# A two-layer trunk on one core: the FFN as two stages with its inner rows in DRAM between them

## Chip, cores, metric

One core of a Trainium2 chip runs one launch of the kernel. The metric is device time in microseconds (us). Engines are named as the profile names them: PE multiplies matrices (PEld loads its weights), DVE, ACT and POOL work on tiles, SP issues most DMAs.

## What is computed

The reference runs two layers over 1024 latent tokens and 128 prompt tokens (T = 1152, that is 9 tiles of 128), with D = 1024. Each layer is a mixer (layer 0: a diagonal state-space part and differential attention; layer 1: a gated short convolution and an RG-LRU) and a gated convolutional FFN. Every part is wrapped in norms:

```python
def _pre(x, m, g, j):
    return rmsnorm(x, g) * (1 + m[:, 3 * j + 1, None]) + m[:, 3 * j, None]

def _post(x, y, m, g, j):
    return x + m[:, 3 * j + 2, None] * rmsnorm(y, g)
```

The FFN multiplies the normed rows by `ffn_w_up` (1024 x 5632), convolves each of the 5632 columns along the tokens with three taps, takes gelu of the first 2816 columns times the others (the inner rows: 22 blocks of 128), and multiplies them by `ffn_w_down` (2816 x 1024). All is float32.

## The kernel before

Every operand of a product is split into a high and a low part of PE's float32 type, and three products (high·high, high·low, low·high) replace one (`mm3`, L81 to L87). Everything up to the output gate of layer 0's mixer, some 790 us, is the same instructions before and after; the change is in `phase_c`, which runs layer 0's `mixer_out`, its FFN, `mixer1` (layer 1's mixer), `mixer_out` again and layer 1's FFN.

- `ffn` (L1349 on) takes one inner block of the 22 at a time: two column blocks of `ffn_w_up`, each in three chunks of 384 to 386 tokens (24 products a chunk, 72 a block), convolution straight from PSUM on ACT (L1371) and DVE (L1374), gelu (L1389), the product of the halves (L1392) and its split into `mh` and `ml` (L1393, L1394).
- `down` (L1410 on) is called for two inner blocks at a time, while the next blocks are in work, and adds two halves of 512 columns for each token tile into nine accumulators `acc` in SBUF (L1420). 
- `ffn_end` (L1424 on) runs over the nine tiles after the last `down`: sum of squares (`junk`, L255), root on POOL (`rsv`, `rs`: L141, L144), scale by the gate table (L1447), add the residual row (L1448), store; in layer 0 also the next norm (square again, root `q`, L277), eight transposes on PE (`tps`, L284), eight identities on ACT that write `h` (L287) and its split on DVE (L289) and POOL (L290).
- `mixer1` (L1468 on) makes 20 column blocks from `w_in_cd` in three chunks of 384. Four of them feed the RG-LRU (`lru_branch`): the block goes through a four-tap convolution (L1485), is split into `xh` and `xl`, and is multiplied by gate matrices into `gps` tiles; sigmoids (L1526), tanh, exp and root on ACT, and a scan along the tokens on DVE (L1547 forwards, L1550 backwards) follow. The buffer of the first gate, `r`, is the same in both directions.
- `mixer_out` multiplies by the output weights (`ops`), then post norm, residual, store, and the FFN's pre norm.

PSUM: four tiles of one bank for `pps` and `ops` (`ps`), two for `dps` and `gps` (`pd`), two for transposes (`pt`). The text of the program gives only dependencies: a scheduler at build time writes each engine's order, and each engine then runs its instructions, and starts its DMAs, strictly in that order.

## Time and profile before

| | us |
|---|---|
| median of 3 runs (2998.35 to 3001.52) | 3000.33 |
| span of the profiled execution | 2997.2 |
| PE busy | 2816.8 (94%) |
| DVE busy | 2035.9 (68%) |
| ACT busy | 1096.7 (37%) |
| PE busy between 800 and 1700 us | 898.67 of 900 |

The span is what the profile covers; it is 3.1 us under the median of the runs. The chain that ended last, followed back, tells what an engine's time is worth: an engine that is busy but not on the chain costs nothing. The granted clock of PE (1.00 is 2.4 GHz, 0.50 is 1.2 GHz) is given for a stretch as a mean.

### The profile page before, as it was taken

What the parts mean: (1) busy time and instruction counts of PE and PEld (TensorE: products, weight loads), DVE (VectorE), ACT (ScalarE), POOL (GpSimd) and SP (SyncE); (2) the same over time, 40 slices, a digit from 0 to 9 for tenths busy, and PEclk for the clock granted to TensorE, in tenths of its full rate; (3) what the DMA queues carried; (4) which work ended last, traced back from release to release, by engine and by line L of the source; (5) the groups of instructions that cost most, each with busy time, mean ns of one, the idle gap of its engine ahead of it and who ended that gap; (6) DMA issues with size and microseconds to landing.
All of it is one profiled execution on the core that took longest, in us unless ns stands there. A gap on an engine that the chain in (4) does not pass through costs nothing.

```text
span 2997.2 us, 40584 instructions
## 1 busy us (share of the span) xinstructions
PE 2816.8 (94%) x15196; PEld 2557.3 (85%) x15196; DVE 2035.9 (68%) x3572; ACT 1096.7 (37%) x1921; POOL 813.7 (27%) x982
## 2 busy tenths in 40 slices
PE   7976788888999999999999989999999999999998
PEld 3874566777789999999999979997899999999997
DVE  6777765988668888888655685455455555555557
ACT  5222113766454222322222365554532222222222
POOL 2699972877131000000000151112300000000001
PEclk9998899999999999999999999999999999999999
DMA  6434447552642333323211131124411111111113
GB/s 222 142 86 107 117 138 200 137 116 75 193 146 89 98 99 96 97 91 93 62 43 57 64 122 55 53 88 146 138 46 43 43 43 43 43 43 43 43 36 134
DMA packets 298835, 279.45 MB, mean 93 GB/s; under 512 B 45454, under 2 KB 259682, under 8 KB 298638
## 3 DMA queue, kind: packets, MB, share of 16 engines
q1 hardware_dynamic: 266168, 238.51, 25.8%
q0 software_dynamic: 14912, 23.21, 3.1%
q10 hardware_dynamic: 17558, 15.14, 1.8%
q8 instruction: 119, 1.95, 0.3%
q14 instruction: 78, 0.64, 0.1%
HBM read 220.59 MB, written 56.20 MB: 92 GB/s over the span
## 4 chain that ended last, share of the span: by engine, by line
PE 69%; DVE 6%; ACT 3%; issue 2%; DMA 1%; POOL 1%; ACTq 0%; DVEq 0%; POOLq 0%; SPq 0%
PE pps L87 43%; PE dps L87 16%; PE ops L87 6%; DVE e L1077 1%; DVE nb L1060 1%; PE sA L1055 1%; ACT e L1066 1%; PE gps L87 1%; PE tps L284 1%; DVE wh L1102 0%; DVE s L1114 0%; PE ops L1145 0%; DMA mw<-w_mod 0%; POOL hl L290 0%; PE gps L759 0%
## 5 line engine op out<-in xcount | busy, mean ns | idle before, releaser
L87 PE MATMUL pps<-hh,whi 128*128 128x384 f32 (+1 forms) x2880 | 977.0, 339 | 1.1 <-ACT whi L97 0.7
L87 PE MATMUL pps<-hh,wlo 128*128 128x384 f32 (+1 forms) x2880 | 974.7, 339 | 2.2 <-DVE wlo L99 2.2
L87 PE MATMUL pps<-hl,whi 128*128 128x384 f32 (+1 forms) x2880 | 974.7, 339 | 0.6 <-POOL hl L798 0.4
L87 PEld LDWEIGHTS pps<-hh,whi 128*128 128x128 f32 x2880 | 546.1, 190 | 17.5 <-issue 3.2
L87 PEld LDWEIGHTS pps<-hh,wlo 128*128 128x128 f32 x2880 | 545.6, 189 | 15.2 <-DVE wlo L99 3.2
L87 PEld LDWEIGHTS pps<-hl,whi 128*128 128x128 f32 x2880 | 546.4, 190 | 8.1 <-DVE hl L798 0.7
L99 POOL TENSOR_TENSOR wlo<-wr,whi 128x1024 fp32r<-128x1024 f32 x44 | 109.2, 2487 | 1455.3 <-PE dps L87 1162.5
L1374 DVE SCALAR_TENSOR_TENSOR cc<-pps,cvc,cc 128x255 f32<-128x255 f32 (+1 forms) x704 | 342.0, 511 | 145.0 <-ACT cc L1371 139.8
L1420 DVE TENSOR_TENSOR acc<-acc,dps 128x512 f32<-128x512 f32 x360 | 245.9, 683 | 232.5 <-PE dps L87 231.5
L1371 ACT ACTIVATE cc<-pps,cvc 128x383 f32<-128x383 f32 (+2 forms) x264 | 175.0, 665 | 414.1 <-PE pps L87 393.3
L87 PE MATMUL dps<-whi,mh 128*128 128x512 f32 x792 | 311.8, 394 | 1.2 <-DVE acc L1420 1.2
L87 PE MATMUL dps<-whi,ml 128*128 128x512 f32 x792 | 312.0, 394 | 0.0
L87 PE MATMUL dps<-wlo,mh 128*128 128x512 f32 x792 | 310.5, 392 | 0.0
L97 ACT ACTIVATE whi<-wr 128x1024 fp32r<-128x1024 f32 x168 | 177.7, 1059 | 278.3 <-PE pps L87 196.6
L99 DVE TENSOR_TENSOR wlo<-wr,whi 128x1024 fp32r<-128x1024 f32 x124 | 153.9, 1243 | 85.4 <-PE pps L87 70.4
L231 DVE SCALAR_TENSOR_TENSOR macc<-mw,sil,macc 128x256 f32<-128x256 f32 x392 | 174.9, 482 | 18.9 <-DMA mw<-w_mod 18.1
L87 PEld LDWEIGHTS dps<-whi,ml 128*128 128x128 f32 x792 | 148.8, 188 | 33.7
L87 PEld LDWEIGHTS dps<-whi,mh 128*128 128x128 f32 x792 | 149.2, 188 | 20.8 <-DVE acc L1420 2.4
L87 PEld LDWEIGHTS dps<-wlo,mh 128*128 128x128 f32 x792 | 149.2, 188 | 18.8
L1389 ACT ACTIVATE cc<-cc 128x385 f32<-128x385 f32 x132 | 69.3, 525 | 248.1 <-DVE cc L1374 232.2
L1104 POOL TENSOR_TENSOR wl<-wf,wh 128x512 fp32r<-128x512 f32 (+2 forms) x96 | 144.4, 1523 | 52.5 <-DVE ra L1074 44.1
L1394 DVE TENSOR_TENSOR ml<-cc,mh 128x385 fp32r<-128x385 f32 x132 | 118.2, 899 | 34.2 <-ACT mh L1393 34.2
(356 smaller groups left out, 4171.6 us busy)
## 6 DMA issues: line engine op xcount, KB each, us to landing
wr<-ffn_w_up SPq DMA_DIRECT2D x88, 512.0 KB
mw<-w_mod SPq DMA_DIRECT2D x224, 128.0 KB
x<-x SPq DMA_DIRECT2D x45, 512.0 KB
wr<-ffn_w_down SPq DMA_DIRECT2D x44, 512.0 KB
wm<-w_mod SPq DMA_DIRECT2D x40, 512.0 KB
k<-kh POOLq DMA_DIRECT2D x8, 1408.0 KB, 6.4
wr<-w_in_cd SPq DMA_DIRECT2D x20, 512.0 KB
yr<-y SPq DMA_DIRECT2D x17, 512.0 KB
```

Of the source, the lines that this page charges most:

```text
L87: nc.tensor.matmul(ps, x, y, start=first and i == 0 and j == 0, stop=last and i == n - 1 and j == 2)
L97: nc.scalar.activation(hi, raw, AF.Copy)
L99: (eng or nc.vector).tensor_tensor(lo, raw, f(hi), op=OP.subtract)
L231: nc.vector.scalar_tensor_tensor(acc[v], wt, s, acc[v], op0=OP.mult, op1=OP.add)
L284: nc.tensor.transpose(ps[:, i], tmp[:, b * 128:(b + 1) * 128], self.id)
L1055: pin(nc.tensor.matmul(A[:, c:c + w], heads[u.h, 2][:, m, u.q0:u.q0 + 128], heads[u.h, m][:, j, u.k0 + c:u.k0 + c + w], start=j == 0, stop ...
L1104: pin((nc.vector if late else nc.gpsimd).tensor_tensor(vl, u.wf[b][:, :k], f(vh), op=OP.subtract))
L1371: nc.scalar.activation(cc[:, :no], ps[:, q:q + no], AF.Identity, bias=cw[3], scale=cw[1])
L1374: nc.vector.scalar_tensor_tensor(cc[:, oa - o0:ob - o0], ps[:, oa + d - i0:ob + d - i0], cw[j], cc[:, oa - o0:ob - o0], op0=OP.mult, op1=O ...
L1389: nc.scalar.activation(cc[:, :no], cc[:, :no], AF.Gelu_apprx_tanh)
L1394: nc.vector.tensor_tensor(ml[:, o0:o1], g[1][:, :no], f(mh[:, o0:o1]), op=OP.subtract)
L1420: nc.vector.tensor_tensor(acc[t][:, sl], acc[t][:, sl], ps, op=OP.add)
```

## The change

The FFN becomes two stages. `up` makes all 22 inner blocks: each column block in two halves of 576 tokens, each half two products of 288 columns for every weight (96 a block), in a PSUM tile of two banks. DVE and ACT copy it to SBUF (tile `C`), the convolution runs from there over all tokens, and the inner rows go to DRAM (`m0`, `m1`), unsplit. `down` then takes groups of 8, 8 and 6 inner blocks. For each group it keeps the split weights in SBUF, and for each tile loads the group's inner rows (`mr`), splits them (`mh` on ACT, `ml` on DVE), and makes all products of the tile in one PSUM tile: 48 matmuls of 512 columns in the first two groups, 36 in the last. Group 0 copies the result to `acc` on ACT, the others add it on DVE (1024 wide). In the last group `finish` is called for each tile: what `ffn_end` did, per tile. The 28 pieces of the modulation, which stood in layer 0's `ffn`, stand 22 in `up` and 6 in group 0 of `down`.

Pools: `big` has 14 tiles (normed rows, split weights of `down`, RG-LRU buffers), `mid` 8, and `wr` 8 tiles, which raw weights, their split pairs in `up`, `mr`, `mh`, `ml`, residual rows, `tmp` and tables share. PSUM: three tiles of two banks for every product (`pps`, `gps`, `ops`, `dps` alike), two for transposes. `mixer1` makes its 20 blocks in the same two halves of 576.

```diff
-    def ffn(self, l, hh, hl, acc, back):
...
-    def down(self, grp, acc, w_down):
...
-    def ffn_end(self, acc, xin, ga, out=None, xout=None, cols=None, hh=None, hl=None):
...
+    def pair(self, raw, eng, pool=None):
+        shape = list(raw.shape)
+        p = (pool or self.wr).tile([128, 2] + shape[1:], F32R, tag="big" if pool else "wr", name=self.nm("wp"))
+        self.nc.scalar.activation(p[:, 0], raw, AF.Copy)
+        eng.tensor_tensor(p[:, 1], raw, f(p[:, 0]), op=OP.subtract)
+        return p
+    def prod(self, prs, ys, name):
+        nc = self.nc
+        ps = self.bank2(name)
+        w = HT // 2
+        steps = [(p[:, x, k], y[j][:, k]) for p, y in zip(prs, ys) for k in range(4) for x, j in ((0, 0), (0, 1), (1, 0))]
+        for n, (x, y) in enumerate(steps):
+            for c in range(2):
+                nc.tensor.matmul(ps[:, c, :w], x, y[:, c * w:c * w + w], start=n == 0, stop=n == len(steps) - 1)
+        return ps[:, :, :w]
...
+    def up(self, l, H, back):
+        nc = self.nc
+        w_up = self.a["ffn_w_up"][l]
         for fb in range(NFB):
+            C = []
+            for b in (fb, NFB + fb):
+                raw = self.load_w(w_up[:, b * 128:b * 128 + 128].rearrange("(k p) c -> p k c", p=128), [128, 8, 128])
+                C.append(self.mid_tile([128, 2, HT], "C"))
+                prs = [self.pair(raw[:, q * 4:q * 4 + 4], (nc.gpsimd, nc.vector)[q]) for q in range(2)]
+                for n in range(2):
+                    pv = self.prod(prs, [H.b[q, n] for q in range(2)], "pps")
+                    if n:
+                        nc.scalar.activation(two(C[-1][:, n]), pv, AF.Copy)
+                    else:
+                        nc.vector.tensor_copy(two(C[-1][:, n]), pv)
+            self.up_rest(l, fb, C)
             if back:
                 self.mod_piece(*back.pop(0))
+    def up_rest(self, l, fb, C):
...
+        nc.vector.tensor_tensor(g[1], g[0], g[1], op=OP.mult)
+        nc.sync.dma_start(self.scratch(f"m{l}", [NFB, 128, T])[fb], g[1])
...
+    GROUPS = (range(0, 8), range(8, 16), range(16, 22))
+    def down(self, l, finish, back):
+        nc = self.nc
+        w_down = self.a["ffn_w_down"][l]
+        m = self.scratch(f"m{l}", [NFB, 128, T])
+        acc = []
+        for gi, fbs in enumerate(self.GROUPS):
+            n = len(fbs)
+            W = []
+            for fb in fbs:
+                W.append(self.pair(self.load_w(w_down[fb * 128:fb * 128 + 128], [128, D]), nc.gpsimd if fb % 2 else nc.vector, self.big))
+            for t in range(NT):
+                raw = self.wr_tile([128, n, 128], "mr")
+                nc.sync.dma_start(raw, m[fbs[0]:fbs[-1] + 1, :, t * 128:t * 128 + 128].rearrange("f p t -> p f t"))
+                hi, lo = (self.wr_tile([128, n, 128], "m" + x, F32R) for x in "hl")
+                nc.scalar.activation(hi, raw, AF.Copy)
+                nc.vector.tensor_tensor(lo, raw, f(hi), op=OP.subtract)
+                ps = self.bank2("dps")
+                for i in range(n):
+                    for j, (x, y) in enumerate(((hi, 0), (lo, 0), (hi, 1))):
+                        for h in range(2):
+                            nc.tensor.matmul(ps[:, h], x[:, i], W[i][:, y, h * 512:h * 512 + 512],
+                                             start=i == 0 and j == 0, stop=i == n - 1 and j == 2)
+                pv = ps.rearrange("p h c -> p (h c)")
+                if gi == 0:
+                    acc.append(self.mid_tile([128, D], "acc") if t < 8 else self.wr_tile([128, D], "acc"))
+                    nc.scalar.activation(acc[t], pv, AF.Copy)
                 else:
+                    nc.vector.tensor_tensor(acc[t], acc[t], pv, op=OP.add)
+                if gi < 2 and back:
+                    self.mod_piece(*back.pop(0))
+                if gi == 2:
+                    finish(t, acc[t])
+    def ffn_fin(self, t, y, xin, ga, out=None, xout=None, cols=None, H=None):
+        nc = self.nc
+        x = self.wr_tile([128, D], "x")
+        nc.sync.dma_start(x, xin[t * 128:t * 128 + 128])
+        tmp = self.wr_tile([128, D], "tmp")
+        rs = self.rstd(self.sumsq([y], tmp), D)
+        nc.vector.scalar_tensor_tensor(y, y, rs, ga[t == 8], op0=OP.mult, op1=OP.mult)
+        nc.vector.tensor_tensor(y, y, x, op=OP.add)
+        nc.sync.dma_start(out(t) if out else xout[t * 128:t * 128 + 128], y)
+        if out is None:
+            self.pre(t, y, tmp, cols, H)
...
         def P(c0, use):
-            self.proj(self.wcol(w, c0), hh, hl, self.ps, "ps", CH, use)
+            raw = self.load_w(w[:, c0:c0 + 128].rearrange("(k p) c -> p k c", p=128), [128, 8, 128])
+            p = self.pair(raw, V, self.big)
+            for n in range(2):
+                use(self.prod([p[:, :, q * 4:q * 4 + 4] for q in range(2)], [H.b[q, n] for q in range(2)], "pps"), n * HT, n * HT + HT)
...
-                    for i0, i1 in CH:
-                        ps = self.pd.tile([128, 512], F32, tag="pd", name=self.nm("gps"))
-                        self.mm3(ps[:, :i1 - i0], [(Wg[0][:, d * 2 + src], Wg[1][:, d * 2 + src])], [(xh[:, i0:i1], xl[:, i0:i1])])
-                        s = A.activation(dst[:, i0:i1], ps[:, :i1 - i0], AF.Sigmoid, bias=col(bc + d * 4 + j))
+                    for n in range(2):
+                        ps = self.bank2("gps")[:, :, :HT // 2]
+                        xv, lv = (two(x[:, n * HT:n * HT + HT]) for x in (xh, xl))
+                        for i, (u, y) in enumerate(((0, xv), (0, lv), (1, xv))):
+                            for c in range(2):
+                                nc.tensor.matmul(ps[:, c], Wg[:, u, d * 2 + src], y[:, c], start=i == 0, stop=i == 2)
+                        s = A.activation(two(dst[:, n * HT:n * HT + HT]), ps, AF.Sigmoid, bias=col(bc + d * 4 + j))
                 t = A.activation(t_, r, AF.Tanh, scale=self.hc[:, d * 4 + j:d * 4 + j + 1])
...
-            self.A = P("A", 1)
-            self.C1, self.wr, self.w, self.whi, self.C2 = P("C1", 1), P("wr", 2), P("w", 4), P("whi", 5), P("C2", 1)
-            self.cv, self.nrm = P("cv", 4), P("nrm", 2)
+            self.big = P("big", 14)
...
-            self.mid = P("mid", 6)
-            self.B = P("B", 1)
-            self.ps = P("ps", 4, space=PSUM)
-            self.pd = P("pd", 2, space=PSUM)
+            self.mid, self.wr = P("mid", 8), P("wr", 8)
+            self.ps = P("ps", 3, space=PSUM)
             self.pt = P("pt", 2, space=PSUM)
...
+            fin = {}
+            def finish0(t, y):
+                if t == 0:
+                    fin["ga"] = [self.table(self.wr, "wr", 0, 5, v) for v in range(2)]
+                    fin["cols"] = self.mod_cols(1, (1, 0), self.wr, "wr", self.pt, "pt", 2)
+                    fin["H"] = Blocks(self, False)
+                self.ffn_fin(t, y, x1, fin["ga"], None, x2, fin["cols"], fin["H"])
             with self.P("mp", 1) as self.mp, self.P("rp", 2) as self.rp:
-                self.ffn(0, hh, hl, acc, back)
+                self.up(0, H, back)
+                self.down(0, finish0, back)
             assert not back
-            self.junk = P("junk", 1).tile([128, D], F32, name="junk")
-            GA = lambda l: [[self.table(self.whi, "whi", l, 5, 0)], [self.table(self.cv, "cv", l, 5, 1, h, 512) for h in (0, 512)]]
-            hh, hl = H()
-            ga = GA(0)
-            cols = self.mod_cols(1, (1, 0), self.nrm, "n", self.pt, "pt", 2)
-            self.ffn_end(acc, x1, ga, None, x2, cols, hh, hl)
...
+            self.up(1, H, [])
+            gb = []
+            def finish1(t, y):
+                if t == 0:
+                    gb.extend(self.table(self.wr, "wr", 1, 5, v) for v in range(2))
+                self.ffn_fin(t, y, x3, gb, lambda t: self.o["o_ys"][0, t * 128:t * 128 + 128] if t < 8 else self.o["o_yp"][0])
+            self.down(1, finish1, [])
```

The order that the scheduler wrote, at three places. First PE in `mixer1`, at the gates of the second RG-LRU block: `pps` are products of a column block, `gps` of a gate matrix, `xh` and `xl` the two parts of the convolved block. Before:

```order
L87 MATMUL pps_18013<-hh_16681,wlo_17985 128x384
L87 MATMUL pps_18013<-hh_16681,whi_17983 128x384
L87 MATMUL gps_17815<-xh_17794,whi_17790 128x384
L87 MATMUL gps_17815<-xl_17795,whi_17790 128x384
L87 MATMUL gps_17815<-xh_17794,wlo_17792 128x384
L87 MATMUL gps_17820<-xh_17794,whi_17790 128x384
L87 MATMUL gps_17820<-xl_17795,whi_17790 128x384
L87 MATMUL gps_17820<-xh_17794,wlo_17792 128x384
L87 MATMUL pps_18013<-hl_16682,whi_17983 128x384
L87 MATMUL pps_18013<-hh_16681,wlo_17985 128x384
L87 MATMUL pps_18013<-hh_16681,whi_17983 128x384
```

After (each row x2 is two matmuls):

```order
L1408 MATMUL pps_18258<-hl_16730,wp_18205 128x288 x2
L1408 MATMUL pps_18258<-hh_16729,wp_18205 128x288 x2
L1578 MATMUL gps_18332<-xh_18321,wp_18318 128x288 x2
L1578 MATMUL gps_18340<-xh_18321,wp_18318 128x288 x2
L1578 MATMUL gps_18348<-xh_18321,wp_18318 128x288 x2
L1578 MATMUL gps_18332<-xl_18322,wp_18318 128x288 x2
L1578 MATMUL gps_18332<-xh_18321,wp_18318 128x288 x2
L1578 MATMUL gps_18340<-xl_18322,wp_18318 128x288 x2
L1578 MATMUL gps_18340<-xh_18321,wp_18318 128x288 x2
L1578 MATMUL gps_18348<-xl_18322,wp_18318 128x288 x2
L1578 MATMUL gps_18348<-xh_18321,wp_18318 128x288 x2
```

Before, the gates stood in pairs among products of other column blocks; now all eight gate tiles of the block stand in one run, directly behind the block that they are made from, and the next column block stands behind the eighth.

Second, DVE in the last products of layer 0's FFN: `L1420` and `L1480` add products to `acc`, `L1447` and `L1493` scale by the gate, `L1448` and `L1494` add the residual row, `L277` and `L297` are the next norm's scaling, `L289` and `L314` the split of the normed rows. Before:

```order
L1420 TENSOR_TENSOR acc_8968<-acc_8968,dps_16565 128x512
L277 TENSOR_SCALAR x_16743<-acc_8968,q 128x1024
L1420 TENSOR_TENSOR acc_8968<-acc_8968,dps_16576 128x512
L277 TENSOR_SCALAR x_16785<-acc_8968,q 128x1024
L1447 SCALAR_TENSOR_TENSOR acc_8968<-acc_8968,rs,tab__2713_16683 128x1024
L1420 TENSOR_TENSOR acc_8968<-acc_8968,dps_16587 128x512
L1448 TENSOR_TENSOR acc_8968<-acc_8968,x_16827 128x1024
L1447 SCALAR_TENSOR_TENSOR acc_8968<-acc_8968,rs,tab__2713_16683 128x1024
```

After:

```order
L1480 TENSOR_TENSOR acc_15420<-acc_15420,dps_16779 128x1024
L1493 SCALAR_TENSOR_TENSOR acc_15420<-acc_15420,rs,tab__2429_16707 128x1024
L1494 TENSOR_TENSOR acc_15420<-acc_15420,x_16817 128x1024
L297 TENSOR_SCALAR tmp_16819<-acc_15420,q 128x1024
L314 CAST hh_16723<-h_16836 128x4x128
L314 CAST hh_16727<-h_16836 128x4x128
L1468 TENSOR_TENSOR ml_16862<-mr_16859,mh_16861 128x768
L1480 TENSOR_TENSOR acc_15528<-acc_15528,dps_16865 128x1024
```

Before, the adds of later products stood among the steps of earlier tiles; now all steps of tile 1 stand ahead of `ml` of tile 2 (L1468), and that ahead of tile 2's add. On SP, in the same place (`L1495` is the store of a tile's rows, `L1465` the load of inner rows, `L1490` that of the residual row):

```order
L1490 DMA x_16817<-x_7943 128x1024
L1495 DMA x_7944<-acc_15420 128x1024
L1465 DMA mr_16859<-m_9146 128x6x128
L1490 DMA x_16903<-x_7943 128x1024
L1495 DMA x_7944<-acc_15528 128x1024
L1465 DMA mr_16945<-m_9146 128x6x128
L1490 DMA x_16989<-x_7943 128x1024
```

The load of tile t + 1's inner rows stands behind the store of tile t. On ACT the eight identities of tile t stand ahead of `mh` of tile t + 1.

Third, DVE in the last group of layer 1's FFN, with the same names. Before:

```order
L1420 TENSOR_TENSOR acc_20337<-acc_20337,dps_26444 128x512
L1448 TENSOR_TENSOR acc_20337<-acc_20337,x_26582 128x1024
L1420 TENSOR_TENSOR acc_20337<-acc_20337,dps_26455 128x512
L1447 SCALAR_TENSOR_TENSOR acc_20337<-acc_20337,rs,tab__3808_26543 128x1024
L1420 TENSOR_TENSOR acc_20337<-acc_20337,dps_26466 128x512
L1448 TENSOR_TENSOR acc_20337<-acc_20337,x_26593 128x1024
L1420 TENSOR_TENSOR acc_20337<-acc_20337,dps_26477 128x512
```

After:

```order
L1468 TENSOR_TENSOR ml_27613<-mr_27610,mh_27612 128x768
L1494 TENSOR_TENSOR acc_26521<-acc_26521,x_27598 128x1024
L1480 TENSOR_TENSOR acc_26578<-acc_26578,dps_27616 128x1024
L1493 SCALAR_TENSOR_TENSOR acc_26578<-acc_26578,rs,tab__3228_27426 128x1024
L1468 TENSOR_TENSOR ml_27669<-mr_27666,mh_27668 128x768
L1494 TENSOR_TENSOR acc_26578<-acc_26578,x_27654 128x1024
L1480 TENSOR_TENSOR acc_26635<-acc_26635,dps_27672 128x1024
```

Here `ml` of the next tile stands behind the scaling (L1493) of the tile before it, ahead of its residual add.

## Rows read from the trace of the kernel before

**Rows 1.** Page, parts 1 and 4: engine busy us (share) xinstructions; chain by line.

```profile
PE 2816.8 (94%) x15196; PEld 2557.3 (85%) x15196; DVE 2035.9 (68%) x3572; ACT 1096.7 (37%) x1921; POOL 813.7 (27%) x982
...
PE pps L87 43%; PE dps L87 16%; PE ops L87 6%; DVE e L1077 1%; DVE nb L1060 1%; PE sA L1055 1%; ACT e L1066 1%; PE gps L87 1%; PE tps L284 1%; DVE wh L1102 0%; DVE s L1114 0%; PE ops L1145 0%; DMA mw<-w_mod 0%; POOL hl L290 0%; PE gps L759 0%
```

**Rows 2.** Stretches: length, busy of each engine (xcount), clock, DMA share, GB/s.

```profile
220.00:240.00 20.00, 9.26 (x73) 7.89 (x73) 16.08 (x22) 3.31 (x8) 19.20 (x28) 0.79 0.29 79
800.00:1700.00 900.00, 898.67 (x4745) 837.14 (x4744) 680.56 (x1315) 289.13 (x515) 94.19 (x76) 1.00 0.28 87
1735.00:1775.00 40.00, 27.16 (x128) 22.33 (x127) 32.22 (x35) 27.48 (x68) 32.62 (x33) 0.83 0.37 132
1775.00:2025.00 250.00, 249.15 (x1437) 248.31 (x1436) 137.34 (x203) 136.71 (x173) 31.77 (x16) 1.00 0.22 69
2025.00:2075.00 50.00, 43.91 (x209) 37.93 (x208) 31.63 (x41) 23.49 (x34) 9.32 (x9) 0.97 0.44 148
```

**Rows 3.** Chain of waits, three places: start us, us, what.

```profile
744.37 3.15 PE gps L759 x24
...
1564.91 24.57 PE pps L87 x140
1589.47 2.76 PE dps L87 x12
...
2075.62 0.87 PE tps L284 x8
2076.50 10.92 PE ops L87 x48
```

**Rows 4.** Chain of waits, one tile's FFN finish in layer 0.

```profile
1707.99 1.16 ACT junk L255 x2
...
1709.23 0.20 POOL rsv L141
...
1709.50 0.55 POOL rs L144
...
1710.08 1.28 DVE acc L1447
```

**Rows 5.** Groups, whole span: busy us, mean ns of one, idle before, releasers.

```profile
L1420 DVE TENSOR_TENSOR acc<-acc,dps 128x512 f32<-128x512 f32 x360 | 245.9, 683 | 232.5 <-PE dps L87 231.5
...
L1448 DVE TENSOR_TENSOR acc<-acc,x 128x1024 f32<-128x1024 f32 x17 | 20.7, 1217 | 0.0
...
L277 DVE TENSOR_SCALAR tmp<-x,q 128x1024 f32<-128x1024 f32 x18 | 13.6, 753 | 46.8 <-POOL q L144 46.8
```

**Rows 6.** Timeline of ACT, mixer_out 1: eight identities of one tile.

```profile
2111.58 2.90 ACT L287 ACTIVATE h<-tps,mc,mc 128x128 f32<-128x128 f32 x8
```

**Rows 7.** Groups, 1778 to 2050 us: RG-LRU work of layer 1's mixer.

```profile
L1526 ACT ACTIVATE L<-gps,lruc 128x384 f32<-128x384 f32 x48 | 26.2, 579 | 36.4 <-PE gps L87 20.7 <-DVE L L1547 15.6
...
L1485 DVE SCALAR_TENSOR_TENSOR L<-t,lruc,L 128x1023 f32<-128x1023 f32 (+3 forms) x24 | 18.0, 813 | 5.3 <-ACT L L1513 5.3
...
L1535 DVE SCALAR_TENSOR_TENSOR L<-L 128x1152 f32<-128x1152 f32 x8 | 11.5, 1442 | 13.2 <-ACT L L1532 13.2
...
L1530 ACT ACT_TABLE_LOAD x8 | 10.3, 1283 | 0.1
...
L1547 DVE TENSOR_TENSOR_SCAN L<-L 128x1152 f32<-128x1152 f32 x4 | 10.2, 2557 | 0.1
...
L1530 ACT ACTIVATE L<-L,nc 128x1152 f32<-128x1152 f32 x8 | 10.1, 1262 | 0.1
...
L1532 ACT ACTIVATE L<-L 128x1152 f32<-128x1152 f32 x8 | 9.4, 1169 | 0.4
...
L1517 DVE TENSOR_TENSOR xl<-L,xh 128x1152 fp32r<-128x1152 f32 x4 | 5.4, 1358 | 3.9 <-ACT xh L1516 3.9
```

**Rows 8.** Chain of waits, start of mixer_out 1: a store and a load.

```profile
2053.67 3.31 DMA y<-t
...
2057.11 5.64 DMA yr<-y
```

More of the change, by code (lines that the diff above doesn't have):

```diff
@@ L24, with two, __init__, raw @@
 CH = ((0, 384), (384, 768), (768, 1152))
-CHF = ((0, 386, 0, 385), (384, 770, 385, 769), (768, 1152, 769, 1152))
+HT = T // 2
 def f(ap):
     return ap.bitcast(F32)
+def two(ap):
+    return ap.rearrange("p (c j) -> p c j", j=HT // 2)
+class Blocks:
+    def __init__(self, k, raws):
+        keys = [(q, n) for q in range(2) for n in range(2) if not (raws and (q, n) == (0, 1))]
+        self.b = {x: [k.big.tile([128, 4, HT], F32R, tag="big", name=k.nm("h" + s)) for s in "hl"] for x in keys}
+        self.r = [k.mid.tile([128, 2, HT], F32, tag="mid", name=k.nm("hr")) for _ in range(2)] if raws else None
+    def raw(self, q, n):
+        return self.r if self.r and (q, n) == (0, 1) else None
+    def parts(self, c0, c1):
+        return [(n, max(c0 - n * HT, 0), min(c1 - n * HT, HT)) for n in range(2) if c0 < n * HT + HT and c1 > n * HT]
 def host_constants():
@@ L1336, in mixer_out @@
                 nc.vector.tensor_tensor(yl[:, s], y, f(yh[:, s]), op=OP.subtract)
-            ps = [self.ps.tile([128, 512], F32, tag="ps", name=self.nm("ops")) for _ in range(2)]
+            ps = self.bank2("ops")
             groups = [[0, 1, 2], [4, 5, 6], [3, 7]] if l and t < 2 else [range(8)]
@@ L1591, in gate_w @@
                     nc.scalar.dma_start(raw[q * 64:q * 64 + 64, d * 2 + s, q * 64:q * 64 + 64], a[nme][0, d, j * 2 + q])
[L1592 removed]
+        return self.pair(raw, nc.vector)
     def phase_c(self, late):
```

224 lines of the change are left out of this document (78 added, 146 removed).

## Prediction

> **What bounds the kernel now.** I read the page's busy times and chain first, then PE and its clock by stretch, then the chain piece by piece. PE is busy 94% of the span, and `pps`, `dps` and `ops` alone are 65% of the chain [rows 1]. From 800 to 1700 us PE idles 1.3 us of 900 at full clock, and in `mixer1` 0.9 of 250; it loses something only where layer 0 ends (12.8 of 40 us idle, clock 0.83) and where the second `mixer_out` begins (6.1 of 50) [rows 2]. DVE and ACT have slack everywhere in between. So the change can win only at those two places or by making PE's own work shorter, and it loses whatever makes PE wait where it now does not.
>
> **PE's own work.** Before, a column block is 72 products at 24.57 / 140 = 0.1755 us, that is 12.64 us. After, it is 96 of 288 columns. A run of that width stands in the gate of layer 0: 3.15 / 24 = 0.131 us [rows 3], so 12.60 us. Over 108 blocks (88 of `up`, 20 of `mixer1`) that is -4 us. The down products stay 2376 of 512 columns; interleaved they take 2.76 / 12 = 0.230, a run of that width alone (`ops`) 10.92 / 48 = 0.2275 [rows 3], -6 us. Together -10; if the rate of the 288-column run were 2% worse, +17, so the bounds are -15 and +20. The convolution, the copies from PSUM and the store and reload of the inner rows lie on DVE, ACT and the queues; for two column blocks (25.2 us of PE) DVE has two copies of half of 1.36, four pairs of taps at 18.0 / 12 = 1.5, the product of 1.36 and two half splits of 0.6 [rows 5, 7], some 10 us, and ACT less; weights are loaded about two inner blocks ahead. They cost nothing in `up` as long as PE stays behind. I cost them at nothing; if DVE's modulation pieces beside them took more than the other 15 us, PE would wait on PSUM.
>
> **Last group of layer 0's down products.** Here the new order puts a whole tile's finish between two tiles of PE's work. After the products of tile t end, and until PE can go on with tile t+1, these follow one another: add of 1024 columns, 2 x 0.683 = 1.37 [rows 5]; square 1.16, root until the next step 0.93 and scale 1.28 [rows 4]; residual add 1.22 [rows 5]; square and root again, 1.16 + 0.93; scale 0.75 [rows 5]; four transposes 0.44 (half of 0.87) [rows 3]; eight identities 2.90 [rows 6]; `mh`, three quarters of a 1024-wide ACT step, 0.87; `ml`, three quarters of 1.22, 0.92. That is 13.9 us, since `ml` of tile t+1 stands behind tile t's steps on DVE and `mh` behind its identities on ACT. The load of tile t+1's inner rows stands behind tile t's store on SP, so it starts at 6.0 and lands, by the store of 3.31 and the load of 5.64 [rows 8], at 9 to 12: hidden by the identities. One pair of matmuls needs `mh` alone; the other 34 take 7.7 us. A tile takes 21.7 us, against 9.1 of PE's work: 12.6 lost, eight times, 101 us. Behind the ninth tile `mixer1`'s first weight is loaded behind the last store, and split behind the identities: 12.1 + 1.2 - 0.9 = 12.4 more. What it replaces is the end of layer 0 now, 12.8 idle plus 17% of 27.2 for the clock, 17.5 us [rows 2]. Net **+96**.
>
> **`mixer1`.** The gates of an RG-LRU block now stand directly behind its column block, and all products share three PSUM tiles. First wait: copy from PSUM 0.7 (between 0.58 for 384 columns and 1.17 for 1152), the affine step 1.26, the taps 18.0 / 4 = 4.5, `xh` 1.17 (as the root of that width), `xl` 1.36 [rows 7], less six matmuls that need only `xh`: 8.2 us. Second wait: the eighth gate tile needs the PSUM tile of the fifth, which the first sigmoid of the other direction empties into `r`, and `r` is still read by the first direction's scan. From the fourth sigmoid on: tanh and exp 1.26 each with a table load of 1.28, then on ACT three weight splits of about 1.16 each and a table load of 1.28 (DVE's step beside them is 1.36), the root 1.17, on DVE 1.44, 0.75, 1.36 and the scan 2.56 [rows 5, 7], the sigmoid 0.7: 16.5, less 0.8 for the seventh tile: 15.7. Now the same scan ends waits of ACT (15.6 us in all) [rows 7], but PE has other blocks' products between the gates. Four blocks of 23.9 are **+96**; without the three splits +82.
>
> **Last group of layer 1.** `ml` of the next tile stands behind the scale of the tile before: 1.37 + 1.16 + 0.93 + 1.28 + 0.92 = 5.7 us, less 0.5 of the first pair [rows 3 to 5], eight times: **+42**. The store and the load two tiles ahead fit in the period of 13.4.
>
> **Boundaries.** From group 0 to group 1 the last weights and the first inner rows wait for tiles that the last matmuls of group 0 free: four loads of 512 KB. Bounds: one load beside two others, 5.64, and four one after another, 4 x 3.31 [rows 8]; then the split of 2.4, less a pair. 7.6 to 15; I take 9, since loads overlap: **+18** for two layers. From `mixer_out` to `up` the first weight is queued behind the ninth tile's store and split behind its identities: 1.16 + 0.93 + 1.28 + 1.16 + 0.93 + 0.75 + 0.44 + 2.90 + 0.6 - 0.9 = 9.3 [rows 4 to 6]: **+19** for two. From `mixer1` to `mixer_out` three steps of split remain, some 3 us, where now 6.1 are lost: **-3**. The tail is the finish of one tile before and after: 0.
>
> **Clock.** Where PE was busy 46% of 20 us its granted clock was 0.79, where 68% of 40 us, 0.83 [rows 2]. In the last group of layer 0 it is busy 42%: at 0.8 its 36 x 0.2275 = 8.2 us per tile grow by 2.0, 16 in all; layer 1's (61%) by 0.9 each, 7; eight waits in `mixer1` at 1.5 are 12. Sum **+35**, an estimate between 0 and 70.
>
> **Sum.** -10 + 96 + 96 + 42 + 18 + 19 - 3 + 35 = +293 on a span of 2997.2: 3290. The median lies 3.1 above the span: **3293**.
>
> The Trainium skill ("Perfetto Trace Analysis", Optimization Strategy) advises to interleave regimes that are limited by different engines, and this change takes them apart. By it the up stage, limited by PE, should have hidden the finishes; the rows agree in so far as the stretch where they are interleaved loses 1.3 us in 900. The sum by rows already contains this.
>
> **Rivals.**
> 1. *The finish is hidden.* If DVE and ACT took the next tile's split ahead of the finish, as the adds do now, a tile would cost 9.1 us, and if the other waits were covered too, only the gains would be left: -10, -17.5 and -6: 2967, faster. It decides where the chain between two tiles falls under 9.1 us instead of 13.9 plus 7.7. Against it: the written order, in which each engine proceeds. 3%.
> 2. *The gates are covered.* `mixer1`'s waits vanish, with their 12 of the clock: 3185. For it: PE before never waited there. Against: the gates stand in one run. 12%.
> 3. *The low clock stays.* If PE ran at 1.2 GHz through every last-group tile and every run of gates, 16 x 8.2 and 4 x 6.3 more, 156 in place of 35: 3414. For it: every wait of 5 to 16 us can end at the low level. Against: with 46% busy the mean was still 0.79 [rows 2]. 9%. The Trainium skill ("TensorE: Matmul & The Clock Gate", HAM oscillation) says that a loop with a gap in each turn pays for the change of clock in every turn; by that rule this rival, or its half, is the one.
> 4. *The change doesn't do this*, since the gates and layer 1's splits come early and only the waits of layer 0's last group stay: 3000 + 96 = 3096. 4%.
>
> **How the numbers follow.** The forecast has 71%. Its own range: without the clock, the splits and with the low boundary, 3230; with twice the clock, boundaries at 15 and the gaps between steps that the durations leave out (0.6 in each of 16 tiles), 3365. 8 in 10 needs rival 2 as well, and some room for waits of either sign that I have not read: **3165 to 3395**. A measurement tells 0.2% (6 us) from no change. Slower holds rivals 2 to 4 and the forecast: 0.96; faster, rival 1, 0.03; 0.01 is left for no change, a time between rivals 1 and 4.
>
> **What would show it.** In the new profile: PE busy near 2800 us but only 85% of the span; `dps` waiting for DVE `ml` in layer 0's last group with tiles 21.7 us apart and in layer 1's 13.4 apart; `gps` waiting for `xl` (8 us) and for a sigmoid (16 us), four times each; 288-column products at 0.131 us; no waits of `pps` in `up`. The prediction is wrong if `dps` follow one another at 9 us in layer 0's last group, if gates run without a gap, or if `pps` wait in `up`.

## The result, and the profile after

The changed kernel takes 3411.56 us (median; 3409.55 to 3416.47) against 2999.34 of the kernel before beside it: a ratio of 1.1378, 95% interval 1.1362 to 1.1394. The direction was forecast, the size was not: 3293 had been predicted, with a range up to 3395. The profiled execution spans 3407.4 us, 410.2 more than before. First the page's busy line, which answers to [rows 1]:

```profile
PE 2914.6 (86%) x17836; PEld 2632.1 (77%) x17836; DVE 1816.8 (53%) x2761; ACT 1106.4 (32%) x1730; POOL 880.0 (26%) x1054
```

PE is busy 97.8 us longer than before (2914.6 less 2816.8), so 410.2 - 97.8 = 312.4 us of the growth is idle time, and 97.8 is PE being slower or having more to do. The stretches tell where, in the columns of [rows 2]: `mixer_out` of layer 0, `up`, groups 0 and 1 of `down`, the last group from about its second tile on, `mixer1`, then the same for layer 1.

```profile
789.40:938.00 148.60, 116.35 (x522) 95.09 (x521) 71.67 (x95) 58.31 (x130) 43.03 (x58) 0.88 0.43 133
938.00:1508.50 570.50, 567.83 (x4299) 567.61 (x4300) 420.90 (x693) 189.68 (x245) 69.94 (x47) 1.00 0.35 109
1508.50:1737.70 229.20, 212.44 (x929) 174.56 (x927) 101.91 (x163) 48.60 (x55) 19.52 (x7) 0.96 0.35 108
1737.70:1948.30 210.60, 101.97 (x362) 77.44 (x361) 59.65 (x71) 55.50 (x125) 41.09 (x56) 0.70 0.20 61
1948.30:2343.50 395.20, 303.20 (x2114) 300.04 (x2114) 157.46 (x212) 144.53 (x155) 35.53 (x17) 0.87 0.16 48
2343.50:2482.00 138.50, 110.67 (x505) 89.77 (x505) 64.05 (x67) 61.12 (x131) 39.44 (x57) 0.91 0.39 125
2482.00:3047.80 565.80, 565.80 (x4224) 565.47 (x4225) 250.38 (x285) 170.46 (x204) 76.93 (x49) 1.00 0.22 71
3047.80:3266.00 218.20, 202.92 (x884) 167.07 (x883) 54.59 (x43) 43.95 (x43) 19.53 (x7) 0.96 0.28 86
3266.00:3398.00 132.00, 93.09 (x307) 69.39 (x305) 36.92 (x33) 15.05 (x24) 5.91 (x16) 0.79 0.26 85
```

Both `up` stages are full, as forecast. Idle time and low clock stand together in the last groups, in `mixer1`, and on either side of `up`. PE's timeline shows the turns (a row is a start, a duration, an instruction, a count; in brackets the idle time ahead of it and who ended it). One tile of layer 0's last group:

```profile
1795.81 1.97 PE L303 MATMUL tps<-misc,tmp 128*128 128x128 f32 x8 [8.97 <-DVE tmp L297]
1800.70 1.22 PE L1473 MATMUL dps<-wp,mh 128*128 128x512 f32 x2 [2.93 <-ACT mh L1467]
1801.72 1.20 PE L1473 MATMUL dps<-wp,ml 128*128 128x512 f32 x2
```

Two waits, 11.9 us a tile, and behind them eight transposes in 1.97 us and pairs of `dps` in 1.2, which take 1.03 and 0.62 at the full clock. One block of `mixer1`, the waits for `xh` and for the first direction's sigmoid buffer:

```profile
1972.69 1.81 PE L1578 MATMUL gps<-xh,wp 128*128 128x288 f32 x6 [7.86 <-ACT xh L1566]
...
1995.92 0.85 PE L1578 MATMUL gps<-xh,wp 128*128 128x288 f32 x2 [14.71 <-ACT L L1579]
```

Behind layer 1's last `ops`, the finishes of three tiles in a row, not of one:

```profile
2455.99 1.49 PE L303 MATMUL tps<-misc,tmp 128*128 128x128 f32 x8 [3.41 <-DVE tmp L297]
2466.45 1.97 PE L303 MATMUL tps<-misc,tmp 128*128 128x128 f32 x8 [8.97 <-DVE tmp L297]
2477.38 1.97 PE L303 MATMUL tps<-misc,tmp 128*128 128x128 f32 x8 [8.96 <-DVE tmp L297]
2482.00 0.85 PE L1408 MATMUL pps<-hh,wp 128*128 128x288 f32 x2 [2.65 <-ACT wp L1396]
```

And one tile of layer 1's last group. After 4.9 us of waiting it takes until 3296.3 before pairs are back at 0.62:

```profile
3288.67 0.73 PE L1473 MATMUL dps<-wp,mh 128*128 128x512 f32 x2 [3.28 <-ACT mh L1467]
3291.04 1.22 PE L1473 MATMUL dps<-wp,ml 128*128 128x512 f32 x2 [1.63 <-DVE ml L1468]
3292.06 1.91 PE L1473 MATMUL dps<-wp,mh 128*128 128x512 f32 x4
3293.76 1.05 PE L1473 MATMUL dps<-wp,ml 128*128 128x512 f32 x2
3294.62 1.82 PE L1473 MATMUL dps<-wp,mh 128*128 128x512 f32 x4
3296.28 0.63 PE L1473 MATMUL dps<-wp,ml 128*128 128x512 f32 x2
```

### The profile page after: what moved, and what is told of

The parts are those of the page before. It is cut to its first block, busy times and chain, and to the rows that moved or that the text cites. A ratio compares the mean times of both kernels' runs of the same rounds, so it can differ in the third digit from the quotient of the medians.

```text
span 3407.4 us, 45146 instructions
## 1 busy us (share of the span) xinstructions
PE 2914.6 (86%) x17836; PEld 2632.1 (77%) x17836; DVE 1816.8 (53%) x2761; ACT 1106.4 (32%) x1730; POOL 880.0 (26%) x1054
## 5 line engine op out<-in xcount | busy, mean ns | idle before, releaser
L1408 PE MATMUL pps<-hh,wp 128*128 128x288 f32 x6912 | 1209.6, 297 | 7.0 <-ACT wp L1396 4.6
L1408 PEld LDWEIGHTS pps<-hh,wp 128*128 128x128 f32 x6912 | 1022.9, 190 | 8.6 <-ACT wp L1396 5.2
L1408 PE MATMUL pps<-hl,wp 128*128 128x288 f32 x3456 | 742.8, 297 | 0.0
L1408 PEld LDWEIGHTS pps<-hl,wp 128*128 128x128 f32 x3456 | 560.3, 190 | 0.0
L1397 POOL TENSOR_TENSOR wp<-wr,wp 128x512 fp32r<-128x512 f32 (+1 forms) x110 | 187.4, 1707 | 1370.4 <-ACT wp L1396 1308.2
L1473 PE MATMUL dps<-wp,mh 128*128 128x512 f32 x1584 | 457.8, 410 | 73.6 <-ACT mh L1467 73.6
L1473 PEld LDWEIGHTS dps<-wp,mh 128*128 128x128 f32 x1584 | 314.1, 200 | 147.6 <-ACT mh L1467 80.9
L1444 DVE SCALAR_TENSOR_TENSOR cc<-C,cvc,cc 128x1023 f32<-128x1023 f32 x352 | 303.3, 917 | 125.7 <-ACT cc L1440 125.6
L1473 PE MATMUL dps<-wp,ml 128*128 128x512 f32 x792 | 261.8, 413 | 20.6 <-DVE ml L1468 20.5
L1480 DVE TENSOR_TENSOR acc<-acc,dps 128x1024 f32<-128x1024 f32 x36 | 43.9, 1221 | 279.6 <-PE dps L1473 279.6
L110 PE MATMUL ops<-Wo,yh 128*128 128x512 f32 x576 | 182.0, 394 | 3.9 <-DVE Wo L1328 3.9
```

The source lines that it names most:

```text
L110: nc.tensor.matmul(ps, x, y, start=first and i == 0 and j == 0, stop=last and i == n - 1 and j == 2)
L1397: eng.tensor_tensor(p[:, 1], raw, f(p[:, 0]), op=OP.subtract)
L1408: nc.tensor.matmul(ps[:, c, :w], x, y[:, c * w:c * w + w], start=n == 0, stop=n == len(steps) - 1)
L1444: nc.vector.scalar_tensor_tensor(cc[:, o0:o1], src[:, o0 + d:o1 + d], cw[j], cc[:, o0:o1], op0=OP.mult, op1=OP.add)
L1473: nc.tensor.matmul(ps[:, h], x[:, i], W[i][:, y, h * 512:h * 512 + 512], start=i == 0 and j == 0, stop=i == n - 1 and j == 2)
```

## The experiments

Each edits the changed kernel at one place, the last ones at several, and is timed beside the kernel before. The changed kernel itself stands at 3411.0 (3408.8 to 3415.4) on the chip of the last comparison.

### Why a tile waits for the one before it

`fin_room` gives the finish other slots (`h` too, which is not shown), and the second half of layer 0's next H (the normed rows, `hh` and `hl`) is taken only at tile 3.

```diff
-        x = self.wr_tile([128, D], "x")
+        new = self.big_tile if t < 3 else self.mid_tile
+        x = new([128, D], "x")
...
-        tmp = self.wr_tile([128, D], "tmp")
+        tmp = new([128, D], "tmp")
```

> Only the last group of down in both layers: the finish's x, tmp and h lie in big (tiles 0 to 2) or in the slots of mid that finished sums have left, no longer in wr, and the second half of layer 0's next H is taken at tile 3. The order that the scheduler writes then has the tps of a tile one to four tiles behind its dps, and mh of tile t+1 ahead of the square of tile t. Theory 1 (of wr's 8 slots 5 were left for mr, mh, ml, x and tmp, so that a tile could only be loaded after the one before it was finished, and this set both periods): layer 0's period falls from 24.3 to 9 to 12 us and layer 1's from 16.1 to 8 to 10, less some 10 to 20 us for the last tiles' finishes at the end of each; the kernel runs in 3240 to 3290. Theory 2 (the finish's engines, ScalarE and VectorE, can't go faster than about 16 us a tile): layer 0 to about 17 us a tile, layer 1 not at all, the kernel runs in 3340 to 3360. Theory 3 (the order is not the cause): within 10 us of 3411.

3264.48 us, ratio 1.088 (1.0864 to 1.0896): 147 us less. Theory 1. Stretches of the last groups (layer 0, the start of `mixer1` behind it, layer 1):

```profile
1737.00:1809.00 72.00, 70.62 (x332) 58.22 (x331) 38.65 (x41) 29.48 (x61) 20.65 (x29) 1.00 0.36 121
1809.00:1866.00 57.00, 17.57 (x87) 14.70 (x85) 24.10 (x27) 26.97 (x67) 18.83 (x28) 0.64 0.36 113
...
3183.00:3247.00 64.00, 63.60 (x281) 52.34 (x279) 34.66 (x31) 13.90 (x22) 5.94 (x16) 1.00 0.46 160
```

The eight tiles behind the first now take 72 us at full clock in layer 0, where they took 196 (1737.7 to 1933.9), and layer 1's group has no gap. So it was the room in `wr` that made PE wait: with the tables and the ninth sum in it, five slots were left for `mr`, `mh`, `ml`, `x` and `tmp`, and with more room the order that the scheduler writes has a tile's `tps` one to four tiles behind its `dps`. No run has that order without the room, so the two are shown together and not apart. 39 us of idle time now stand behind the group, where 12 stood, for the last tiles' finishes come before `mixer1` (17.57 busy in 57). The Trainium skill ("Perfetto Trace Analysis", Optimization Strategy) says that the same gap repeating can mean that there is no room for the next tile; these runs agree.

### What the low clock costs

`warm` and `warm2` add products on weights that lie ready to layer 0's last group, into a PSUM tile that nobody reads, to fill its waits. In `warm` the scheduler chose their places and 72 went in per tile; `warm2` fixes them.

```diff
+                        ws = [nc.tensor.matmul(wp[:, i >= 70, :288], W[i % n][:, 0, 512:640], W[i % n][:, 0, :288], start=True, stop=True)
+                              for i in range(92)]
```

> Only layer 0's last group: behind the dps of each of its nine tiles 72 products of 288 columns on weights that lie ready, into a tile of pt that nobody reads; they fill about 9 of the 11.9 us in which TensorE waits for tmp and mh. They add work and take no wait away. Theory 1 (the waits cost more than their idle time, since the granted clock, 0.70 in this stage, makes the 36 dps of a tile some 3 us slower): the clock of the stage rises to 0.95 or more, each dps runs at its full rate, the period falls from 24.3 to 21 to 22 us, the kernel runs in 3380 to 3395. Theory 2 (the clock costs nothing at the end of the stage, the period hangs on the finish chain alone): period 24 us, within 5 us of 3411. Theory 3 (the added products delay the tps and the mh's dps): slower by up to 9 x 3 us, 3420 to 3440.

> Layer 0's last group again with 92 added products of 288 columns per tile on weights that lie ready, now in a tile of their own and in a fixed place: 70 between the last dps of a tile and its tps (70 x 0.134 = 9.4 us, where TensorE waited 8.96 for tmp), 22 between the tps and the next tile's dps (2.9 us, where it waited 2.92 for mh). In the first attempt 26 of them stood behind an idle gap, ran at half rate and held up the dps. Theory 1 (each turn of the wait costs, beside its idle time, 1.8 us of dps and 0.9 of tps at the 1.2 GHz level, since the clock falls in it): no product of the group runs at the low level any more, the period falls from 24.3 to 21.5 to 22 us, the kernel runs in 3385 to 3397. Theory 2 (the clock isn't paid at the end of the period): 24.3 us and 3405 to 3417.

`warm`: 3424.23 us, ratio 1.1413 (1.1394 to 1.1432), theory 3. Its timeline shows that 26 of the added products waited for the transposes' PSUM tile, ran at half rate and held the `dps` up:

```profile
1800.39 1.09 PE L304 MATMUL tps<-misc,tmp 128*128 128x128 f32 x8 [3.32 <-DVE tmp L298]
1802.70 6.34 PE L1488 MATMUL warm<-wp 128*128 128x288 f32 x26 [1.22 <-ACT h L311]
1808.88 0.63 PE L1474 MATMUL dps<-wp,mh 128*128 128x512 f32 x2
```

`warm2`: 3387.71 us, ratio 1.129 (1.1273 to 1.1307), 23 less with 828 products more. A turn of it, and then its stretch of 200 us:

```profile
1808.17 9.38 PE L1493 MATMUL warm<-wp 128*128 128x288 f32 x70
1817.38 1.03 PE L303 MATMUL tps<-misc,tmp 128*128 128x128 f32 x8
1818.17 3.15 PE L1493 MATMUL warm<-wp 128*128 128x288 f32 x22
1821.76 0.73 PE L1477 MATMUL dps<-wp,mh 128*128 128x512 f32 x2 [0.45 <-ACT mh L1471]
```

```profile
1737.00:1937.00 200.00, 191.62 (x1211) 174.09 (x1210) 59.74 (x68) 55.55 (x125) 42.02 (x57) 1.00 0.21 65
```

The clock is 1.00 where it was 0.70, and the period 22.4 us (1799.3 to 1821.8) where it was 24.2: theory 1, a little short of its 21.5 to 22. No wait is shorter; what went is 1.2 us of the transposes and 1.5 of the `dps`, less 0.9 by which the added products overrun the waits. Of the 28 us by which the profiled execution is shorter, 14 lie here (from the end of `up` to `mixer1`'s first product, 428.8 us for 443.1), 2 in `mixer1` and 14 in layer 1's `up`, which has nothing to do with the edit (last section); 2 were lost before. Without that `up` the profiled execution would have taken some 3396, still theory 1. The Trainium skill ("TensorE: Matmul & The Clock Gate", HAM oscillation) says that a loop with a gap in every turn pays for the clock in every turn; the trace agrees, at 2.7 us a turn in this group.

### `mixer1`

`m1_apart` makes the two branches generators and sets conv blocks between the gates; `m1_apart2` copies the weights' high halves on DVE besides (the last four lines). The places in the branches where they hand over are not shown.

```diff
-            lru_branch(j)
-            conv_branch(j)
+            b, c = lru_branch(j), conv_branch(j)
+            for x in (b, c, b, c, b, c) if j < 3 else (b, c, b, b, c, c):
+                next(x, None)
...
-            p = self.pair(raw, V, self.big)
+            p = self.big.tile([128, 2] + list(raw.shape)[1:], F32R, tag="big", name=self.nm("wp"))
+            V.tensor_copy(p[:, 0], raw)
+            V.tensor_tensor(p[:, 1], raw, f(p[:, 0]), op=OP.subtract)
```

> Only mixer1 is written in another order: of each of its four blocks the gate products of the two directions stand apart, with at least one or two blocks of pps between them, and the first stands behind pps too. Theory 1 (the 22.6 us of idle TensorE in each block, 7.86 for xh and 14.71 for the sigmoid of the direction before, come from the place of the gates in the order): the waits go, 4 x 22.6 = 90 us less a few us at the last block, and the stage's granted clock rises from 0.87 to over 0.95, which is worth some 15 us more; the stage shrinks from 395 us to 285 to 310, the kernel runs in 3300 to 3330. Theory 2 (ScalarE and VectorE set mixer1's period of 97.2 us whatever the order, by their sigmoids, tables and scans): the idle time moves to the pps or to other gates, the stage stays over 370 us, the kernel runs in 3385 to 3415.

> The kernel with mixer1's gates set apart, and beside that the high half of each of mixer1's weights copied on VectorE in place of ScalarE. In the run before, 43 us of idle time were left in mixer1: 5.49 and 3.07 us in each block for a weight's high half, which stood behind four sigmoids, tanh, exp and two table loads in ScalarE's queue. Theory 1 (that queue is what is left): most of the 4 x 8.6 us go, 25 to 35 us with the clock; 3310 to 3340. Theory 2 (VectorE's scans and taps then hold the weights up as long, or the slots of big do): within 10 us of 3361.

`m1_apart`: 3360.97 us, ratio 1.1191 (1.116 to 1.1222), 50 less, between the two theories. The gates' waits are gone to 0.4 us each, but two new ones are there in each block, both for a weight's high half on ACT:

```profile
2051.53 0.53 PE L1408 MATMUL pps<-hh,wp 128*128 128x288 f32 x2 [3.07 <-ACT wp L1396]
...
2069.61 0.53 PE L1585 MATMUL gps<-xh,wp 128*128 128x288 f32 x2 [0.40 <-ACT L L1586]
...
2076.16 0.85 PE L1408 MATMUL pps<-hh,wp 128*128 128x288 f32 x2 [5.49 <-ACT wp L1396]
```

What came back is idle time alone: the stage's granted clock rose from 0.87 to 0.92, not over 0.95, and PE is busy 305.5 us in it where it was 303.2. `m1_apart2`: 3342.99 us, ratio 1.1139 (1.1122 to 1.1155). The waits for ACT are gone, and DVE's turn comes:

```profile
2059.36 0.53 PE L1587 MATMUL gps<-xh,wp 128*128 128x288 f32 x2 [0.40 <-ACT L L1588]
...
2067.06 0.82 PE L1408 MATMUL pps<-hh,wp 128*128 128x288 f32 x2 [6.64 <-DVE wp L1542]
```

`mixer1` took 397.1 us (from the end of the last group to the first `ops`), 345.5 and now 328.0. So the gates' waits come from their place in the order (theory 1 of `m1_apart`), but of the 94 us of idle time and some 19 of clock in this stage 69 came back and not all (62 idle, 7 busy): a weight split is next in the queue of whatever engine makes it. Of the 25 to 35 us that `m1_apart2` was to bring, 18 came.

### Behind `mixer_out`

Three edits for one place. `out_room` keeps one block of H unsplit in `mid` so that no cast waits for an output weight's slot; `out_early` reads two output weights for the last time 36 products sooner; `out_pipe` writes the post norm of a tile ahead of the next norm of the one before. In this order:

```diff
-            H = Blocks(self, False)
+            H = Blocks(self, True)
             self.mixer_out(0, W, self.xsrc, x1, H)
+            H.fill(self)
...
-            groups = [[0, 1, 2], [4, 5, 6], [3, 7]] if l and t < 2 else [range(8)]
+            groups = [[0, 1, 2], [4, 5, 6], [3, 7]] if l and t < 2 else [[0, 1], range(2, 8)] if t == 8 else [range(8)]
...
-            self.pre(t, x, tmp, cols, H)
+            if t:
+                self.pre(t - 1, *last, cols, H)
+            last = x, tmp
+        self.pre(8, *last, cols, H)
```

> Only mixer_out: block (0,1) of H is kept unsplit in two slots of mid until all output rows are done and is split afterwards, so that no hh or hl of tokens 576 and up waits for a slot of big that an output weight holds. Theory 1 (the 25 to 30 us of idle TensorE behind layer 0's ops and 24 behind layer 1's come from tiles 6, 7 and 8 being finished in a row after the last ops frees the slots): one to two tiles' finishes less, 9 to 18 us at each place and some us of clock; the kernel runs in 3375 to 3395. Theory 2 (the chain of the last tiles is as long without that wait, since VectorE and ScalarE are late, or the split of the kept block stands in the way in its place): within 8 us of 3411.

> Only the last tile of mixer_out in both layers: its products go over the output blocks 0 and 1 for both halves first and over 2 to 7 then, so that two of the eight output weights are read for the last time 36 products (8 us) sooner. Theory 1 (hh and hl of block (1,1) wait for the slots of big that output weights hold, and VectorE, which stands at that cast, holds the finishes of tiles 6 and 7 up behind it): the casts come 8 us sooner and the idle time behind the last ops falls by 7 to 9 us in each layer (25 and 24 before), the kernel runs in 3390 to 3400. Theory 2 (the finishes of the last tiles follow one another 10.9 us apart whenever the slots come): no change of that idle time, 3407 to 3417.

> Only mixer_out in both layers: the square, scale and residual add of tile t are written ahead of the next norm (second square, tmp, tps, identities, splits) of tile t-1, so that on ScalarE the square of a tile no longer stands behind the identities of the tile before. Theory 1 (the 10.9 us from tile to tile behind the last ops are one chain of ScalarE, GpSimd and VectorE, in which a tile's square waits in ScalarE's queue for the identities of the tile before, and three such chains stand in a row): two tiles are left behind the last ops, their chains overlap, the idle time there falls from 25 and 24 us to 10 to 16 each, the kernel runs in 3380 to 3398. Theory 2 (the slots of big alone hold these tiles up, and a tile more in flight makes that worse): 24 us or more remain, 3405 to 3425.

`out_room`: 3426.29 us, ratio 1.1414 (1.1394 to 1.1434), 15 slower. Behind the last `ops` of layer 0 the idle time is 13 us where it was 26, and in layer 1 14 where it was 24, as theory 1 has it, but the two slots of `mid` are now missing in the middle of the stage (layer 0):

```profile
857.72 1.97 PE L311 MATMUL tps<-misc,tmp 128*128 128x128 f32 x8 [4.84 <-DVE tmp L305]
868.66 1.97 PE L311 MATMUL tps<-misc,tmp 128*128 128x128 f32 x8 [8.97 <-DVE tmp L305]
875.72 1.22 PE L118 MATMUL ops<-Wo,yh 128*128 128x512 f32 x2 [5.09 <-ACT yh L1373]
...
925.79 1.09 PE L311 MATMUL tps<-misc,tmp 128*128 128x128 f32 x8 [1.77 <-DVE tmp L305]
936.35 1.97 PE L311 MATMUL tps<-misc,tmp 128*128 128x128 f32 x8 [9.46 <-DVE tmp L305]
```

`out_early`: 3410.83 us, ratio 1.1371 (1.1354 to 1.1388), theory 2: the cast came some 5 us sooner and nothing moved. ACT's timeline there shows the chain: the square of a tile (`tmp<-ops`) stands between two sets of identities of the tile before.

```profile
2466.34 1.50 ACT L310 ACTIVATE h<-tps,mc,mc 128x128 f32<-128x128 f32 x4 [2.50 <-issue]
2467.73 1.03 ACT L278 ACTIVATE tmp<-ops 128x1024 f32<-128x1024 f32 x1
...
2473.16 1.06 ACT L278 ACTIVATE tmp<-x 128x1024 f32<-128x1024 f32 x1 [2.91 <-DVE x L290]
...
2477.27 1.50 ACT L310 ACTIVATE h<-tps,mc,mc 128x128 f32<-128x128 f32 x4 [2.97 <-PE tps L303]
2478.66 1.04 ACT L278 ACTIVATE tmp<-ops 128x1024 f32<-128x1024 f32 x1
```

From square to square it is 10.9 us here, and 10.5 from the tile before. `out_pipe`: 3379.41 us, ratio 1.1258 (1.1234 to 1.1282), 32 less: theory 1, at the low end of its range. What is left behind layer 1's `ops` is one chain:

```profile
2447.51 1.97 PE L303 MATMUL tps<-misc,tmp 128*128 128x128 f32 x8 [7.68 <-DVE tmp L297]
...
2452.20 0.85 PE L1411 MATMUL pps<-hh,wp 128*128 128x288 f32 x2 [2.72 <-ACT wp L1399]
```

So the finishes stood in a row because of the order, in which a square waits in ACT's queue; the slots of `big` hold a tile up too (`out_room`), but freeing two of them sooner (`out_early`) moved nothing as long as that order stood.

### All of them

`combo` has `fin_room`, `m1_apart2`, `out_early`, and the first tile of group 1 split ahead of that group's weights; `combo2` has `out_pipe` in place of `out_early`. `again` is the changed kernel itself. What is new in the first two:

```diff
+            first = rows(0) if gi == 1 else None
+            for fb in fbs:
+                W.append(self.pair(self.load_w(w_down[fb * 128:fb * 128 + 128], [128, D]), nc.gpsimd if fb % 2 else nc.vector, self.big))
...
+                hi, lo = first if first and t == 0 else rows(t)
```

> All edits that take a wait away, together: mixer1's gates apart and its weights' high halves on VectorE; the last groups' finish in big and mid; the last tile of mixer_out with two weights freed sooner; and in both layers the first tile of group 1 loaded and split ahead of that group's weights. Theory 1 (the waits are independent of one another, each costs its idle time and some clock): 147 for the last groups, 50 to 90 for mixer1, 10 to 20 for mixer_out, and 10 us less at each start of group 1, where TensorE waits 15.5 now; together 3120 to 3200, still above the kernel before, since the products of 288 columns cost some 30 us more and the last tiles' finishes are left. Theory 2 (a wait that goes is given back at the next place, since the finish of a tile takes 11 us whatever surrounds it): over 3230.

> The kernel with all edits together, but in mixer_out the order in which the square, scale and residual add of tile t come ahead of the next norm of tile t-1 in place of the last tile's earlier weights. If mixer_out's tail is a chain in ScalarE's queue, 10 us less in each layer and 3130 to 3155; if it is the slots, 3160 to 3175 as before.

> The changed kernel once more, with nothing edited. In two of the nine profiles taken so far layer 1's up, which is the same code in all of them, took 552 us (0.130 us for a product of 288 columns), in seven 565 to 566 (0.134), each at a granted clock of 1.00, with no idle time. Theory 1 (this is a state of the single execution): executions of this kernel differ by up to 14 us, around 3398 or 3411. Theory 2 (the edits before it set the state): all of them lie within 5 us of 3411.

`combo`: 3165.91 us, ratio 1.0533 (1.0505 to 1.0561), theory 1; `combo2`: 3133.68, ratio 1.0444 (1.0423 to 1.0466), the chain in ACT's queue. The gains add up: 147 + 68 + 32 are 247 of 277, and the start of group 1, which waits 4.3 us instead of 15.5 in layer 0 and 3.4 instead of 15.3 in layer 1 of `combo`, is most of the rest (layer 0's 15.5 are 11.04 for `mh` and 4.51 for `ml`). In the changed kernel three things end there one behind the other. On ACT eight weights stand ahead of the first `mh`, which then waits another 1.03 for its rows; their load stands behind eight loads of weights on SP. On DVE the first `ml` stands behind the weights' low halves, which end last:

```profile
1613.91 7.68 ACT L1396 ACTIVATE wp<-wr 128x1024 fp32r<-128x1024 f32 x8 [0.27 <-DVE bm L198]
1622.62 1.06 ACT L1467 ACTIVATE mh<-mr 128x1024 fp32r<-128x1024 f32 x1 [1.03 <-DMA mr<-m]
```

```profile
1616.89 9.23 DVE L1397 TENSOR_TENSOR wp<-wr,wp 128x1024 fp32r<-128x1024 f32 x3 [0.67 <-ACT wp L1396]
1626.04 4.50 DVE L1468 TENSOR_TENSOR ml<-mr,mh 128x1024 fp32r<-128x1024 f32 x2
```

The edit moves the load and both splits ahead at once, so what each of the three costs alone is not shown.

Still 4% slower than the kernel before: from 780 us on `combo2` idles 115 us, the kernel before 23. No run here beats it. `again`: all four executions lie within 5 us of 3411, 3408.8 to 3415.4, the time of theory 2.

## Why the prediction was wrong, step by step

The forecast's sum against the trace, in us (span; the first two rows and the clock from PE's busy time and the intervals between products at full clock, the rest idle time):

| step | predicted | measured |
|---|---|---|
| PE's own work | -10 | about +10 |
| products that end ahead of a wait | 0 | about +13 |
| last group, layer 0, and behind it | 101 + 12 | 97 + 12 idle |
| `mixer1` | 96 | 91 idle |
| last group, layer 1 | 42 | 39 idle |
| group 0 to 1, two layers | 18 | 31 idle |
| `mixer_out` to `up`, two layers | 19 | 50 idle |
| `mixer1` to `mixer_out` | 3 | 3 idle |
| idle time before that goes | -19 | -23 |
| elsewhere (inside `mixer_out`, `up`, the first 790 us) | 0 | 13 idle |
| clock, less what the kernel before lost by it (5; 11) | 30 | about 74 |
| sum | 292 | 410 |

**Right** were the four waits and their chains. Layer 0's turn: 11.9 idle where 12.6 was worked out, by the chain of the finish (8.97) and `mh` (2.93). `mixer1`: 22.6 a block where 23.9. Layer 1's turn: 4.9 where 5.2. Each is within 7%, from rows of the kernel before alone. That rivals 1 and 2 did not come true was well judged too, though `fin_room` shows that rival 1, in the last groups, is just what a few more slots bring.

**The clock** was the largest miss, 44 us. The step took a mean clock from two stretches and applied it to the `dps`, and took 1.5 for each wait in `mixer1`, for which it named no row. In the trace, the products behind these waits run at the 1.2 GHz level, the transposes too: layer 0's tile loses 0.9 on `tps` (1.97 for 1.03) and 2.0 on `dps` (36 in 10.2 for 8.2), 8 x 2.9 = 23 where 16 was taken; layer 1's tile takes 11.2 for 36 products that need 8.2, and eight of them lose some 20 to the clock where 7 was taken from the group's busy share; `mixer1`'s 2112 products take 303.2 where they need some 282, and some 19 of that is clock, 2.4 a wait for 1.5. The boundaries, for which nothing was taken, make up the rest. `warm2` shows that this is paid: 2.7 of the 2.9 went with the low clock. Rival 3 names 3414 and the time came out at 3411, but not by its way: it had 156 us of clock, and the trace has some 85.

**From `mixer_out` to `up`** the step priced one tile's finish, 9.3. That price is near (`out_pipe` leaves 10.4 in layer 1 and 11.3 in layer 0), the count was wrong: three tiles stood there, since 14 slots of `big` hold eight output weights and only six of H's eight tiles, and ACT's order let the chains follow one another. 31 us.

**PE's own work.** In layer 0 the price of a column block was right: 12.65 us (96 products at 0.132) for 12.64, and 0.1755 [rows 3] does stand for the FFN's chunks before. But the one rate of 0.131, from 24 gate products, was taken for all 108 blocks, and the one of 0.1755 too. Layer 1's `up` took 0.133 a product; in `mixer1` the 384-column products before ran at 0.173, 12.5 a block, and the new ones take 12.8:

```profile
1800.00:2000.00 200.00, 200.00 (x1156) 200.00 (x1155) 105.39 (x127) 106.38 (x130) 25.14 (x11) 1.00 0.23 73
```

That is 14 us more, and the `down` products gave back some 9 where 6 was forecast; the rest of the +10 is spread too thin to place. No term was there for the ends: the last product ahead of a wait is busy 0.39 us and not the 0.2275 to the next start, and from 780 us on there are over 50 such places more. 20 and 13 us.

**Group 0 to 1** was taken at 9 of 7.6 to 15 and came out at 15.5: the high end, four loads one after another, was near, but the weights' splits ahead of `mh` on ACT and of `ml` on DVE, of which the step counted one, end there too. 13 us.

Together 44 + 31 + 33 + 13 = 121; three waits came out 12 shorter, and 13 of small ones with 4 less of the old idle time leave 118, what was missing. All four go the same way. The range's high end had twice the clock and boundaries at 15, but the clock (85 against 70) and the start of group 1 came out beyond their high ends together, and the three tiles behind `mixer_out` and the ends ahead of waits were in no bound. Its own range is added up wrongly besides: the terms that it names give 3241 and, with every boundary at 15, some 3360, not 3230 and 3365, which changes nothing here.

## What to carry to other kernels

Before a change takes an interleaved schedule apart, count the slots that each pool has left at the tightest place; a shortage shows as the same gap in every turn, and room there was worth more than any change of the written order that was tried (147 us by `fin_room`, against 68 by `m1_apart2` and 32 by `out_pipe`). Price a recurring wait as its idle time plus what PE loses at the low level behind it, 2 to 3 us a turn here, on whatever it runs next. And where a tail is priced, ask how many tiles are in flight when it begins, not only how long one takes.
